# Eight weight low parts moved from GpSimd to VectorE, and an order for the accumulations, in an MLP of split fp32 products

## The chip, the cores and the metric

The kernel runs on one core of a Trainium2 chip. The metric is device time in microseconds for one execution of the program, from inputs in device memory to the output there. A core has TensorE (PE, matrix products into PSUM), VectorE (DVE), ScalarE (ACT), GpSimd (POOL) and SyncE (SP, which issues the DMAs here). Each engine takes its instructions in order; they wait for one another through semaphores.

## The reference

A decoder trunk of two layers on 512 tokens of width 1024, in fp32: a mixer (attention in layer 0, a gated short convolution in layer 1), an MLP and a gated embedding, each with RMSNorm before and after. The change lies in the MLP, which is the same in both layers:

```python
def sq_relu_mlp(h, w_up, w_down):
    return jnp.square(jax.nn.relu(h @ w_up)) @ w_down   # h 512x1024, w_up 1024x4096, w_down 4096x1024

def reference(...):
    for i in range(DEPTH):                              # DEPTH = 2
        ...
        f = sq_relu_mlp(rmsnorm(x, g[2]), w_mlp_up[i], w_mlp_down[i])
        x = x + rmsnorm(f, g[3])
        ...
```

## The kernel before

**Three products for one.** Every fp32 operand is split into a high part, rounded to the format in which TensorE multiplies, and a low part, the rest. ScalarE casts the high part (L272), another engine subtracts it from the source (L273). A product is then three matmuls, high x high (L264), low x high (L265) and high x low (L266), into the same PSUM bank. In the trace the names end in `h` and `l`: `wh`, `wl` for weights, `hTh`, `hTl` for the normed tokens, `A11h`, `A11l` and so on for activations. Which of the matmul's operands is streamed differs, so L265 is `wh` with an activation's low part in the down product and `wl` in the up product.

**Groups.** The 4096 hidden features go in eight groups of 512 (`gr` = 0 to 7), each of four tiles of 128 features (`f`). For each group `up` computes the up product, and ScalarE takes the relu `r` out of the bank (L820) and squares it into `q` (L806). In group 0 the up product runs in two passes of 256 tokens each, so that it can start before all tokens are normed; in the others in one pass of 512.

**Seven products for eight.** For groups 0 to 6 the down product is done with Strassen's seven products in Winograd's form, on 2 x 2 blocks: tokens by halves and hidden features by halves (f = 0, 1 and f = 2, 3) for the activations (A11, A12, A21, A22), hidden features and output columns for the weights (B11 to B22). It needs sums of the activations, S1 to S4, and of the weights, T1 to T4. The products are `PRODUCTS`, run in the order `STEPS`:

```python
PRODUCTS = {
    1: ("A11", "B11"), 2: ("A12", "B21"), 3: ("S4", "B22"), 4: ("A22", "T4"),
    5: ("S1", "T1"), 6: ("S2", "T2"), 7: ("S3", "T3"),
}
STEPS = (1, 2, 4, 5, 6, 7, 3)
```

- GpSimd makes the sums of the weights (`dn_T`, in `derive`, L167) from raw weights that a DMA loaded, T1, T3, T2, T4 for each of two feature tiles (`p` = 0, 1).
- `prepare` splits each weight: ScalarE casts, and the low part is taken by the engine that L185 chooses: GpSimd for every sum of weights in the MLP (keys that begin with `"dn"`), VectorE for plain weights.
- GpSimd makes the sums of the activations (`s`, in `quarters`, L834), for f = 1 and again for f = 3. ScalarE casts them (`S1h`, which holds S1 and S2, then `S3h`, which holds S3 and S4), and VectorE takes their low parts (`S1l`, `S3l`); `A12h` and `A12l` hold A12 and A22. These splits are made in `halves`.
- `down` runs the seven products, each for two halves of 128 tokens (`s` = 0, 1), each in a bank of its own. In group 0 ScalarE copies the banks into the accumulators `acc` (L863); in groups 1 to 6 VectorE adds the banks to `acc` (L866). Only then is a bank free. There are eight banks, taken in turn: the relu `r` of the last up tiles frees the banks for products 5, and the copy or addition of product 1 frees those for product 6.

**Order.** The program is written stage by stage, but outside of a few stretches written by hand a scheduler orders each engine's instructions by a simulated timeline. So an edit can move instructions of other engines, too. `tc.add_manual_dep` with `NoSync` gives the scheduler an order between two instructions of one engine, and adds no semaphore.

Of the kernel before, what the change touches and what calls it, by code (L numbers as in the profile page):

```python
# [8 lines left out]
F32 = mybir.dt.float32  # L9
F32R = mybir.dt.float32r  # L10
AF = mybir.ActivationFunctionType
ALU = mybir.AluOpType
# [42 lines left out]
ON_POOL = ('S3', 'S4')  # L55
# [13 lines left out]
def trunk(ctx: ExitStack, tc, x, pT, g, wv, wqk, bf, wo, wci, wcq, cw, wco, wup, wdn, wpp, wpg, out):  # L69
    nc = tc.nc  # L70
# [9 lines left out]
    def page(name, dtype=F32):  # L80
        return pages.tile([P, S], dtype, tag="pg", name=name)

    def bank(name):
        return psum.tile([P, S], F32, tag="ps", name=name)
# [66 lines left out]
    def fetch(upto):  # L151
        while len(fetched) < min(upto, len(loads)):
            n = len(fetched)
            raw = raws.tile([P, S], F32, tag="raw", name=f"raw{n}")
            fetched.append(raw)
            src = loads[n]
            nc.sync.dma_start(raw[:, : src.shape[-1]], src)

    def derive(key):
        at, sums = recipes.pop(key)  # L160
        fetch(max(at.values()) + 1)
        B = {name: fetched[n][:, :S] for name, n in at.items()}
        for name, a, b, op in sums:
            t = page("_".join(str(u) for u in (*key, *name)))
            derived[(*key, *name)] = t
            B[name] = t[:, :S]
            ins = nc.gpsimd.tensor_tensor(out=B[name], in0=B[a], in1=B[b], op=op)  # L167
            if last_norm:
                tc.add_manual_dep(
                    ins.ins, last_norm.pop().ins.name,  # L170
                    mybir.DependencyInfo(mybir.DependencyClass.Sync, mybir.DependencyReason.DATA),
                )

    def prepare(upto):
        while begun[0] < min(upto, len(order)):
            n = begun[0]
            begun[0] += 1
            key, at = order[n]
            for of in (key[:3], key[:2]):
                if of in recipes:  # L180
                    derive(of)
            hi, lo = page(f"wh{n}", F32R), page(f"wl{n}", F32R)
            if isinstance(at, tuple):
                raw, w = derived.pop(key), S
                eng = nc.gpsimd if key[0] == "dn" or key[-1] in ON_POOL else nc.vector  # L185
            else:
                fetch(at + 1)
                raw, eng, w = fetched[at], nc.vector, loads[at].shape[-1]
                fetched[at] = None
            split(hi[:, :w], lo[:, :w], raw[:, :w], eng)  # L190
            ready[key] = Pair(hi[:, :w], lo[:, :w])

    def wide(*key, soon=SOON):

        prepare(where[key] + 1 + soon)
        return ready[key]
# [6 lines left out]
    for l in range(2):  # L203
# [10 lines left out]
        else:  # L214
# [3 lines left out]
            for i in range(2, KT, 2):  # L218
                for name in "ucb":
                    s = "cub".index(name)  # L220
# [41 lines left out]
    def mm3(ps, a, b, start, stop):  # L262

        nc.tensor.matmul(ps, a.hi, b.hi, start=start, stop=False)  # L264
        nc.tensor.matmul(ps, a.lo, b.hi, start=False, stop=False)  # L265
        nc.tensor.matmul(ps, a.hi, b.lo, start=False, stop=stop)  # L266
        streamed[0] += 3 * ps.shape[-1]
        due()

    def split(hi, lo, src, eng=nc.vector):  # L270

        nc.scalar.copy(hi, src)  # L272
        eng.tensor_tensor(out=lo, in0=src, in1=hi.bitcast(F32), op=ALU.subtract)  # L273

    def gain(l, i):
        ts = [page(f"g{l}_{i}_{n}") for n in range(2)]
# [38 lines left out]
    def keep(t, n, ps, hT):  # L315
        to = lambda h: h[:, 4 * n : 4 * n + 4, t * P : (t + 1) * P]
        split(to(hT.hi), to(hT.lo), ps.rearrange("p (j c) -> p j c", j=4))
# [70 lines left out]
    def attention(hT, first_x, g0, by_hand):  # L388
# [8 lines left out]
        def logs():  # L397

            e, u, lg = stat("f_e", n_f), stat("f_u", n_f), stat("f_l", n_f)
            neg = stat("f_n", n_f)  # L400
            nc.vector.tensor_scalar(out=neg, in0=logit, scalar1=-1.0, scalar2=None, op0=ALU.mult)
            nc.vector.tensor_tensor(out=neg, in0=logit, in1=neg, op=ALU.min)
            nc.scalar.activation(e, neg, AF.Exp)
            nc.vector.tensor_scalar(out=u, in0=e, scalar1=1.0, scalar2=None, op0=ALU.add)
            nc.scalar.activation(lg, u, AF.Ln)
            rest, ru = stat("f_r", n_f), stat("f_ru", n_f)
            nc.vector.scalar_tensor_tensor(
                out=rest, in0=u, scalar=-1.0, in1=e, op0=ALU.add, op1=ALU.subtract
            )
            nc.vector.reciprocal(ru, u)  # L410
            nc.vector.tensor_tensor(out=rest, in0=rest, in1=ru, op=ALU.mult)
            nc.vector.tensor_tensor(out=lg, in0=lg, in1=rest, op=ALU.subtract)
            logf = stat("logf", n_f)
            nc.vector.scalar_tensor_tensor(
                out=logf, in0=logit, scalar=0.0, in1=lg, op0=ALU.min, op1=ALU.subtract
            )
            split(lf.hi, lf.lo, logf)
# [178 lines left out]
        def stream():  # L596
            for i in range(1, KT):
                yield from project(i)
            yield from out_part((0,), range(6))
            yield from out_part((1,), range(6))  # L600
            prepare(where["o", 1, KT - 1] + 1)
            yield from out_part((0, 1), (6,))
# [197 lines left out]
        return lambda k, t: tokens_of(ys[k], t)  # L800

    def mlp(l, hT, xs, then, late):
        acc = {}

        def square(out, r):
            nc.scalar.activation(out, r, AF.Square)  # L806
# [16 lines left out]
        def halves(gr, f, names, src, A):  # L823

            w = S // 2 * len(names)
            part = Pair(*(page(f"{names[0]}{s}{l}_{gr}_{f}", F32R) for s in "hl"))
            split(part.hi[:, :w], part.lo[:, :w], src[:, :w])
            for name, c in zip(names, (slice(0, S // 2), slice(S // 2, S))):
                A[name, f // 2] = part.at(lambda h: h[:, c])

        def quarters(gr, f, q, s, A):

            L, R = slice(0, S // 2), slice(S // 2, S)
            sums = lambda out, a, b, op: nc.gpsimd.tensor_tensor(out=out, in0=a, in1=b, op=op)  # L834
            if f % 2 == 0:
                s[f] = page(f"s34{l}_{gr}_{f}")
                sums(s[f][:, L], q[f][:, L], q[f][:, R], ALU.subtract)
                return
            left, right = q[f - 1], q[f]
            halves(gr, f, ("A12", "A22"), right, A)  # L840
            s12, s34 = page(f"s12{l}_{gr}_{f}"), s[f - 1]
            sums(s12[:, L], left[:, R], right[:, R], ALU.add)
            sums(s12[:, R], s12[:, L], left[:, L], ALU.subtract)
            sums(s34[:, R], right[:, L], s12[:, R], ALU.subtract)
            halves(gr, f, ("S1", "S2"), s12, A)
            halves(gr, f, ("S3", "S4"), s34, A)

        def down(gr, A):

            for i in STEPS:  # L850
                a_name, b_name = PRODUCTS[i]
                banks = [bank(f"dn{l}_{gr}_{i}{s}") for s in range(2)]
                for p in range(2):
                    w = wide("dn", l, gr, b_name, p)
                    for s in range(2):
                        mm3(
                            banks[s], A[a_name, p].at(lambda h: h[:, s * P : (s + 1) * P]), w,
                            p == 0, p == 1,
                        )
                for s in range(2):  # L860
                    if gr == 0:
                        acc[i, s] = page(f"acc{l}_{i}_{s}")
                        nc.scalar.copy(acc[i, s][:, :S], banks[s])  # L863
                    else:
                        a = acc[i, s][:, :S]
                        nc.vector.tensor_tensor(out=a, in0=banks[s], in1=a, op=ALU.add)  # L866

        def combine():

# [9 lines left out]
        for gr in range(7):  # L879
            A, s, q = {}, {}, {f: page(f"q{l}_{gr}_{f}") for f in range(4)}  # L880

            def done(f, lo, hi, r):
                square(q[f][:, lo:hi], r[:, : hi - lo])
                if lo == 0 and f % 2 == 0:
                    halves(gr, f, ("A11",), q[f], A)
                if hi == S:
                    quarters(gr, f, q, s, A)

            up(gr, done)
            down(gr, A)  # L890
# [16 lines left out]
        for t in range(NB):  # L907
            banks = [bank(f"dn{l}_7_{t}_{n}") for n in range(2)]
            for f, n in [(f, n) for f in range(4) for n in range(2)] if t == 0 else [
                (f, n) for n in range(2) for f in range(4)  # L910
            ]:
                w = wide("dn", l, 7, n, f, soon=14)
                mm3(banks[n], tokens_of(hs[f], t), w, f == 0, f == 3)
            for n in range(2):
                a = total[t, n][:, :S]
# [69 lines left out]
    for l in range(2):  # L985
# [16 lines left out]
        def late():  # L1002
# [6 lines left out]
            return g3  # L1009

        mlp(l, h2, xs, lambda t: pre_norm(t, xs[t], g4, hT, f"n4{l}"), late)
        h4 = hT
        g5 = gain(l, 5)
# [88 lines left out]
```

## Time and profile before

| | |
|---|---|
| median of 3 runs (lowest, highest) | 1234.35 us (1234.16, 1234.91) |
| the profiled execution: time, span | 1234.05 us, 1232.3 us |
| granted TensorE clock in it | 0.998 |
| instructions | 18654 |
| busy TensorE / VectorE | 1211.7 us (98%) / 898.9 us (73%) |
| busy ScalarE / GpSimd | 676.6 us (55%) / 680.3 us (55%) |

The span goes from the first to the last instruction of the program; the profiled execution's time is 1.75 us longer. Busy time of TensorE is a union of overlapping matmuls: where one starts before the last has ended, the distance of their starts tells how fast it runs, and not the duration of one. In the rows of a timeline the first number is the start in us from the start of the span, the second the time that the row covers; then engine, line, operation, output <- inputs, partitions x elements, and the number of instructions merged in the row. Brackets give the engine's idle time before the row, and whose work ended it. The MLP of layer 0 starts at about 259 us; group 0's down product runs from 285 to 306, group 1's from 328 to 348. Layer 1's follow some 570 us later.

### The profile page before, as it was taken

The page shows a single profiled execution, that of the slowest core. Times are in us where ns is not written, and L with a number is a line of the kernel's source. Part 1 is how long each engine was busy: PE and PEld are TensorE (multiplying, and loading weights), DVE is VectorE, ACT ScalarE, POOL GpSimd, SP SyncE. Part 2 cuts the span into 40 slices and gives each one's busy share as a digit, 9 for nine tenths or more (in the row PEclk, how much of TensorE's full clock was granted, in tenths as well). Part 3 has the DMA queues.
Part 4 walks back from the last instruction along what each step waited for, and adds up shares of the span by engine and source line. Part 5 has one row for each costly group of instructions (what it writes and reads, how often), then busy time and mean ns, then how long its engine had stood idle before and what let it go on. Part 6 is the DMA issues. An engine that isn't in the chain of part 4 may idle for free.

```text
span 1232.3 us, 18654 instructions
## 1 busy us (share of the span) xinstructions
PE 1211.7 (98%) x6188; PEld 1029.5 (84%) x6188; DVE 898.9 (73%) x1394; ACT 676.6 (55%) x1429; POOL 680.3 (55%) x635
## 2 busy tenths in 40 slices
PE   7999999999999999999999999999999999999997
PEld 6888888898788888888889999989878888888886
DVE  5658878675688767869877798865674787669873
ACT  5457778557634654455566534445756445635551
POOL 2016657147977787775213255317778868778210
PEclk9999999999999999999999999999999999999999
DMA  7456555532343224428123033552421443235401
GB/s 256 151 156 170 151 161 122 188 117 85 96 137 111 85 78 137 134 68 301 53 95 112 27 103 97 161 170 69 137 81 57 137 137 96 67 113 179 163 18 52
DMA packets 85793, 148.73 MB, mean 121 GB/s; under 512 B 10112, under 2 KB 17328, under 8 KB 85696
## 3 DMA queue, kind: packets, MB, share of 16 engines
q1 hardware_dynamic: 85488, 147.27, 39.0%
q8 instruction: 49, 0.80, 0.3%
q14 instruction: 48, 0.39, 0.1%
q10 hardware_dynamic: 144, 0.26, 0.1%
q0 software_dynamic: 64, 0.00, 0.0%
HBM read 136.93 MB, written 6.37 MB: 116 GB/s over the span
## 4 chain that ended last, share of the span: by engine, by line
PE 91%; DVE 3%; ACT 2%; POOL 2%; DMA 1%; issue 1%; SPq 0%; DVEq 0%; POOLq 0%; ACTq 0%
PE up L266 9%; PE up L265 9%; PE up L264 9%; PE dn L265 8%; PE dn L266 8%; PE dn L264 8%; PE qk L265 2%; PE qk L264 2%; PE qk L266 2%; PE pg L265 2%; PE pg L266 2%; PE pg L264 2%; PE pT L539 1%; PE n_p L312 1%; PE co L264 1%; PE co L265 1%
## 5 line engine op out<-in xcount | busy, mean ns | idle before, releaser
L273 DVE TENSOR_TENSOR wl<-raw,wh 128x512 fp32r<-128x512 f32 (+1 forms) x398 | 372.4, 980 | 27.3 <-ACT wh L272 26.2
L272 ACT CAST wh<-raw 128x512 fp32r<-128x512 f32 (+1 forms) x398 | 217.5, 619 | 4.6 <-DVE xd L348 4.4
L266 PE MATMUL up<-hTl,wh 128*128 128x512 f32 (+1 forms) x576 | 209.7, 366 | 0.6 <-DVE hTl L273 0.6
L265 PE MATMUL up<-hTh,wl 128*128 128x512 f32 (+1 forms) x576 | 210.2, 365 | 0.0
L264 PE MATMUL up<-hTh,wh 128*128 128x512 f32 (+1 forms) x576 | 209.4, 366 | 0.0
L273 POOL TENSOR_TENSOR wl<-dn_T,wh 128x512 fp32r<-128x512 f32 x112 | 154.7, 1414 | 32.6 <-ACT wh L272 32.6
L820 ACT ACTIVATE r<-up 128x512 f32<-128x512 f32 (+1 forms) x72 | 39.5, 548 | 199.2 <-PE up L266 199.2
L866 DVE TENSOR_TENSOR acc<-dn,acc 128x512 f32<-128x512 f32 x168 | 107.2, 679 | 23.5 <-PE dn L266 23.5
L266 PEld LDWEIGHTS up<-hTl,wh 128*128 128x128 f32 x576 | 108.3, 189 | 18.2 <-DVE hTl L273 0.8
L264 PEld LDWEIGHTS up<-hTh,wh 128*128 128x128 f32 x576 | 108.7, 189 | 17.6
L265 PEld LDWEIGHTS up<-hTh,wl 128*128 128x128 f32 x576 | 108.6, 189 | 17.5
L167 POOL TENSOR_TENSOR dn_T<-raw,raw 128x512 f32<-128x512 f32 x56 | 87.9, 1582 | 59.8 <-DMA raw<-in_wdn 49.7
L167 POOL TENSOR_TENSOR dn_T<-raw,dn_T 128x512 f32<-128x512 f32 x56 | 92.7, 1656 | 2.2
L272 ACT CAST wh<-dn_T 128x512 fp32r<-128x512 f32 x112 | 61.4, 616 | 11.1 <-POOL dn_T L167 11.1
L273 DVE TENSOR_TENSOR A12l<-q,A12h 128x512 fp32r<-128x512 f32 x28 | 23.6, 844 | 50.2 <-ACT A12h L272 50.2
L273 DVE TENSOR_TENSOR A11l<-q,A11h 128x256 fp32r<-128x256 f32 x28 | 25.6, 914 | 45.9 <-ACT A11h L272 45.9
L873 POOL TENSOR_TENSOR acc<-acc,acc 128x512 f32<-128x512 f32 x28 | 46.9, 1709 | 9.9 <-DVE acc L866 9.9
L265 PE MATMUL qk<-hTh,wl 128*128 128x512 f32 x128 | 51.0, 399 | 0.0
L266 PE MATMUL qk<-hTl,wh 128*128 128x512 f32 x128 | 51.0, 398 | 0.0
L264 PE MATMUL qk<-hTh,wh 128*128 128x512 f32 x128 | 50.9, 398 | 0.0
L265 PE MATMUL pg<-wh,hTl 128*128 128x512 f32 x128 | 50.5, 394 | 0.0
L264 PE MATMUL pg<-wh,hTh 128*128 128x512 f32 x128 | 50.4, 394 | 0.0
(370 smaller groups left out, 3231.5 us busy)
## 6 DMA issues: line engine op xcount, KB each, us to landing
raw<-in_wup SPq DMA_DIRECT2D x128, 256.0 KB, 3.1
raw<-in_wdn SPq DMA_DIRECT2D x128, 256.0 KB, 2.9
raw<-in_wcq SPq DMA_DIRECT2D x36, 256.0 KB, 2.8
raw<-in_wqk SPq DMA_DIRECT2D x32, 256.0 KB, 3.8
raw<-in_wpg SPq DMA_DIRECT2D x32, 256.0 KB, 4.6
g<-in_g SPq DMA_DIRECT2D x22, 256.0 KB, 6.2
prl<-neg_c SPq DMA_DIRECT2D x16, 256.0 KB, 7.0
raw<-in_wo SPq DMA_DIRECT2D x16, 256.0 KB, 5.8
```

The source lines that it names most:

```text
L167: ins = nc.gpsimd.tensor_tensor(out=B[name], in0=B[a], in1=B[b], op=op)
L264: nc.tensor.matmul(ps, a.hi, b.hi, start=start, stop=False)
L265: nc.tensor.matmul(ps, a.lo, b.hi, start=False, stop=False)
L266: nc.tensor.matmul(ps, a.hi, b.lo, start=False, stop=stop)
L272: nc.scalar.copy(hi, src)
L273: eng.tensor_tensor(out=lo, in0=src, in1=hi.bitcast(F32), op=ALU.subtract)
L312: nc.tensor.transpose(ps[:, j * P : (j + 1) * P], h[:, j * P : (j + 1) * P], ident)
L539: nc.tensor.transpose(ps[:, b * P : (b + 1) * P], probs[h][b][:, j * P : (j + 1) * P], ident)
L820: nc.scalar.activation(r[:, :n], ps[:, :n], AF.Relu)
L866: nc.vector.tensor_tensor(out=a, in0=banks[s], in1=a, op=ALU.add)
L873: nc.gpsimd.tensor_tensor(out=a, in0=a, in1=acc[i, s][:, :S], op=ALU.add)
```

## The change

Two edits, in both layers.

1. In `prepare`, the low parts of the sums of weights in group 0 (`key[2]` is the group) are taken by VectorE and no longer by GpSimd: T1 to T4, for two tiles each, eight instructions of 128 x 512 per layer. In groups 1 to 6 they stay on GpSimd.
2. `split` hands back its low part's instruction, and `halves` keeps the last one of each group (`lows[gr]`: the `S3l` of f = 3). In group 1 each of the 14 accumulations on VectorE is ordered behind it. Before, the scheduler had placed `A12l`, `S1l` and `S3l` of f = 3 between the accumulations of products 1, 2 and 4.

```diff
@@ prepare
-                eng = nc.gpsimd if key[0] == "dn" or key[-1] in ON_POOL else nc.vector
+                eng = nc.gpsimd if (key[0] == "dn" and key[2] > 0) or key[-1] in ON_POOL else nc.vector
@@ split
         nc.scalar.copy(hi, src)
-        eng.tensor_tensor(out=lo, in0=src, in1=hi.bitcast(F32), op=ALU.subtract)
+        return eng.tensor_tensor(out=lo, in0=src, in1=hi.bitcast(F32), op=ALU.subtract)
@@ mlp
-        acc = {}
+        acc, lows = {}, {}
@@ halves
-            split(part.hi[:, :w], part.lo[:, :w], src[:, :w])
+            lows[gr] = split(part.hi[:, :w], part.lo[:, :w], src[:, :w])
@@ down
                         a = acc[i, s][:, :S]
-                        nc.vector.tensor_tensor(out=a, in0=banks[s], in1=a, op=ALU.add)
+                        ins = nc.vector.tensor_tensor(out=a, in0=banks[s], in1=a, op=ALU.add)
+                        if gr == 1:
+                            tc.add_manual_dep(
+                                ins.ins, lows[gr].ins.name,
+                                mybir.DependencyInfo(
+                                    mybir.DependencyClass.NoSync, mybir.DependencyReason.DATA
+                                ),
+                            )
```

## The prediction

> **What bounds the kernel now.** I read the page first, then the chain of waits, and then the timeline of each engine around the two groups that the diff touches. The page's first part:
>
> ```profile
> span 1232.3 us, 18654 instructions
> PE 1211.7 (98%) x6188; PEld 1029.5 (84%) x6188; DVE 898.9 (73%) x1394; ACT 676.6 (55%) x1429; POOL 680.3 (55%) x635
> ```
>
> TensorE is the bound. Nothing done on VectorE, ScalarE or GpSimd can shorten the kernel except where TensorE stands still for it. So the question is how many such places there are in the first two MLP groups, and how long they are. In the timeline the first column is the start, the second the duration, and brackets give the idle time before and who ended it. TensorE, down products of group 0, layer 0 and then layer 1:
>
> ```profile
> 290.27 0.39 PE L266 MATMUL dn<-wl,A12h 128*128 128x512 f32 x1
> 291.58 0.50 PE L264 MATMUL dn<-wh,S1h 128*128 128x512 f32 x1 [0.92 <-ACT r L820]
> 292.87 0.39 PE L266 MATMUL dn<-wl,S1h 128*128 128x512 f32 x1
> 293.41 0.73 PE L264 MATMUL dn<-wh,A12h 128*128 128x512 f32 x2 [0.15 <-ACT A12h L272]
> 297.39 0.39 PE L266 MATMUL dn<-wl,S1h 128*128 128x512 f32 x1
> 297.72 0.50 PE L264 MATMUL dn<-wh,S1h 128*128 128x512 f32 x1
> 861.35 0.39 PE L266 MATMUL dn<-wl,A12h 128*128 128x512 f32 x1
> 861.98 0.50 PE L264 MATMUL dn<-wh,S1h 128*128 128x512 f32 x1 [0.24 <-ACT r L820]
> 863.27 0.40 PE L266 MATMUL dn<-wl,S1h 128*128 128x512 f32 x1
> 863.80 0.73 PE L264 MATMUL dn<-wh,A12h 128*128 128x512 f32 x2
> ```
>
> Matmuls overlap: a steady one shows 0.39 but the next starts about 0.23 later (below, three starting at 334.81 end at 335.65, so 0.84 = 2 x 0.23 + 0.39). The loss is therefore the distance of two starts less 0.23, and more than the bracket says. The first after a halt takes 0.50 instead of 0.39, another 0.11. Layer 0 loses 1.08, 0.31 and 0.10, each with 0.11: 1.82 us. Layer 1 loses 0.40 and 0.30, with 0.11 each: 0.92. Group 1, both layers:
>
> ```profile
> 334.81 0.84 PE L264 MATMUL dn<-wh,A12h 128*128 128x512 f32 x3
> 335.79 0.50 PE L265 MATMUL dn<-wh,A12l 128*128 128x512 f32 x1
> 337.75 0.61 PE L264 MATMUL dn<-wh,S1h 128*128 128x512 f32 x2
> 338.75 0.50 PE L265 MATMUL dn<-wh,S1l 128*128 128x512 f32 x1 [0.39 <-DVE S1l L273]
> 339.79 0.39 PE L264 MATMUL dn<-wh,S1h 128*128 128x512 f32 x1
> 905.22 0.84 PE L264 MATMUL dn<-wh,A12h 128*128 128x512 f32 x3
> 906.43 0.50 PE L265 MATMUL dn<-wh,A12l 128*128 128x512 f32 x1 [0.37 <-DVE A12l L273]
> 908.39 0.63 PE L264 MATMUL dn<-wh,S1h 128*128 128x512 f32 x2
> 909.39 0.50 PE L265 MATMUL dn<-wh,S1l 128*128 128x512 f32 x1 [0.38 <-DVE S1l L273]
> ```
>
> Three matmuls from 334.81 make the next due at 335.50; it came at 335.79: 0.29. Two from 337.75 make the next due at 338.21; it came at 338.75: 0.54. With 0.11 each, layer 0 loses 1.05. Layer 1, in the same way, 0.52 + 0.54 + 0.22 = 1.28. Group 1 loses 2.33 us in all.
>
> **Edit 1: eight low parts per layer from GpSimd to VectorE (group 0).** In the built order GpSimd drops two runs of four `wl`; VectorE takes the first four between the `A11l` of f = 0 and that of f = 2, the other four behind `S3l` of f = 3. ScalarE's and SyncE's orders stay as they are, so no cast and no DMA issue is moved. What that does to the path is read from ScalarE, GpSimd and VectorE:
>
> ```profile
> 286.55 0.42 ACT L806 ACTIVATE q<-r 128x256 f32<-128x256 f32 x1
> 289.80 0.62 ACT L272 CAST S1h<-s 128x512 fp32r<-128x512 f32 x1 [2.18 <-POOL s L834]
> 292.29 0.42 ACT L806 ACTIVATE q<-r 128x256 f32<-128x256 f32 x1
> 294.71 0.62 ACT L272 CAST S1h<-s 128x512 fp32r<-128x512 f32 x1 [1.35 <-POOL s L834]
> 856.93 0.42 ACT L806 ACTIVATE q<-r 128x256 f32<-128x256 f32 x1
> 860.20 0.62 ACT L272 CAST S1h<-s 128x512 fp32r<-128x512 f32 x1 [2.19 <-POOL s L834]
> 862.68 0.42 ACT L806 ACTIVATE q<-r 128x256 f32<-128x256 f32 x1
> 865.11 0.62 ACT L272 CAST S1h<-s 128x512 fp32r<-128x512 f32 x1 [1.36 <-POOL s L834]
> ```
> ```profile
> 278.75 3.18 POOL L167 TENSOR_TENSOR dn_T<-raw,dn_T 128x512 f32<-128x512 f32 x2
> 281.88 5.24 POOL L273 TENSOR_TENSOR wl<-dn_T,wh 128x512 fp32r<-128x512 f32 x4
> 287.08 0.74 POOL L834 TENSOR_TENSOR s<-q 128x256 f32<-128x256 f32 x1
> ```
> ```profile
> 275.85 3.48 DVE L273 TENSOR_TENSOR wl<-raw,wh 128x512 fp32r<-128x512 f32 x2
> 279.25 1.51 DVE L273 TENSOR_TENSOR A11l<-q,A11h 128x256 fp32r<-128x256 f32 x1
> 284.81 1.15 DVE L273 TENSOR_TENSOR A11l<-q,A11h 128x256 fp32r<-128x256 f32 x1 [4.05 <-ACT A11h L272]
> 296.18 0.69 DVE L273 TENSOR_TENSOR S3l<-s,S3h 128x512 fp32r<-128x512 f32 x1
> 300.72 1.63 DVE L273 TENSOR_TENSOR wl<-raw,wh 128x512 fp32r<-128x512 f32 x1 [3.85 <-ACT wh L272]
> ```
>
> The chain goes: GpSimd does four `wl` until about 287.1, and only then its sums `s`; ScalarE, in order, stands at the cast `S1h` for them; behind that cast are queued `S3h` and the relu `r` of the next up bank; TensorE waits at 291.58 for just that bank. Take the four `wl` away and `s` waits for `q` alone. What that is worth I read from the second pass of the same code (f = 3), where GpSimd is free: from the end of `q` (292.29 + 0.42 = 292.71) to `S1h` at 294.71 it takes 2.00 us. In the first pass (f = 1) it takes 289.80 - 286.97 = 2.83. Gain 0.83. In layer 1: 2.01 (863.10 to 865.11) against 2.85 (857.35 to 860.20). Gain 0.84.
>
> All that follows on ScalarE in this group moves with it, as its order is fixed: the relus, the casts `A12h` (TensorE's wait at 293.41) and the copies `acc` that free the banks (297.72). In layer 0 the first halt shrinks by 0.83 and the two others stay: gain 0.83. In layer 1 the first halt (0.40) goes, and the rest of the 0.84 comes out of the second: gain 0.84. Sum of edit 1: 1.67 us.
>
> Its cost: eight low parts at 0.69 (the `S3l` row) are 5.5 us of VectorE per layer. The first four need 2.8 in a gap that runs from 280.76 (279.25 + 1.51) to 284.81, 4.05 long; the last four 2.8 in one from 296.87 to 300.72, 3.85 long. I price them at nothing: the gaps cover them. If the cover were gone the next low part would be late by what sticks out. One thing is not covered: GpSimd's last `dn_T` now has a `wl` on VectorE beside it. Side by side both engines run at the same pace (two `wl` in 3.48), and two `dn_T` took 3.18 here, so it might stretch by up to 0.30, and ScalarE, which stands at the cast of that `dn_T`, with it. Between 0 and 0.30 per layer I take 0: this `dn_T` started before the `A11l` ended, so its turn came ahead of any later `wl`. The Trainium skill (SBUF — State Buffer, section "SBUF: two separate sides") says that a GpSimd operation and a VectorE one with two SBUF inputs hold a shared port in turn, each for its whole instruction, whoever starts first; by that rule the term is 0 here, by the pace of the rows up to 0.30, so the sum would be 4.0 or 3.4. The equal pace in the rows agrees with it.
>
> **Edit 2: accumulations of group 1 behind `S3l`.** VectorE now stands idle for a matmul while finished inputs wait behind:
>
> ```profile
> 333.65 1.29 DVE L866 TENSOR_TENSOR acc<-dn,acc 128x512 f32<-128x512 f32 x2 [5.19 <-PE dn L266]
> 332.67 0.62 ACT L272 CAST S3h<-s 128x512 fp32r<-128x512 f32 x1 [0.21 <-POOL s L834]
> ```
>
> It is idle 5.19 us until product 1 is complete, adds it twice, and only then takes up `A12l`; the next accumulation again holds up `S1l`. In the new order all three low parts lie in that idle time: the last cast, `S3h`, ends at 333.29, so `S3l` ends by about 334.0, and TensorE wants `A12l` at 335.50 and `S1l` at 338.21 (334.7 and 337.0 once edit 1 and the first two halts are off), `S3l` later. All four halts go: 2.33 us. What is added is that the accumulations wait for `S3l`: the first starts at 334.0 instead of 333.65, 0.35 late. Behind it are the other accumulations and the `wl` of the next up weights; for its bank waits product 6, whose first matmul was at 339.79. Even brought forward by 1.9 (0.83 and 1.05) that is 337.9, almost 4 us after that start. So no cost. The built order also pulls a few first matmuls of group 2's up product forward over rests of products 7 and 3; nothing is added, and what they read was cast long before. No cost, and bounded by the 2.33 that this edit gives.
>
> **Sum.** 1.67 + 2.33 = 4.00 us off the profiled execution's 1234.05 (span 1232.3) gives 1230.05; the median 1234.35 is 0.3 above that execution, so 1230.3, or 0.33% faster. What a measurement of this kernel can tell from no change is 0.2%, 2.5 us.
>
> **Rivals.**
> - *VectorE takes the port first.* If the first moved `wl` runs ahead of the last `dn_T`, ScalarE is held up by 0.69 in each layer, and edit 1 keeps 0.29: 1231.7. The equal pace, one each in turn, speaks against it. Chance 0.07.
> - *Edit 1 gains nothing*, because ScalarE's next wait ends as late as before: 1234.35 - 2.33 = 1232.0. Against it: in the second pass nothing else ended later. Chance 0.05.
> - *Edit 2 gains nothing*, since a bank's release by the later accumulations takes the place of the low parts: 1232.7. Against it: 4 us of slack. Chance 0.06.
> - *Both work and a later stage takes it back*, as something that TensorE does not pace (weights by DMA) sets a later start: 1234.3. For it: SyncE's order is unchanged. Against it: TensorE at 98%, and the tail hangs on TensorE. Chance 0.06.
> - *VectorE becomes the bound (slower).* If the moved low parts run at the shared pace of 1.74 (3.48 for two), the second four start at 296.87 and end at 303.8, less the 0.83 of the earlier start 303.0, 2.3 past the 300.72 at which the next weights' `wl` began, and TensorE waits. It decides once they end past 300.72 and TensorE has no slack left. Price 2 x 2.3 less edit 2's 2.33: +2.3, 1236.6; where the backlog reaches group 1's low parts too, 1238.9. For it: VectorE is the second busiest engine. Against it: GpSimd, relieved of the same work, has nothing to contend with there. Chance 0.08, counted as slower.
>
> That the change does nothing is no case: the orders of both engines do differ as the diff says.
>
> **Numbers.** Forecast as summed: chance 0.68, at 1230.3. Its own range runs from 1229.0 (all of 1.82 + 0.92 + 2.33 = 5.07 gone, and a little more where layer 1 has a third halt) to 1230.9 (0.30 lost in each layer). The range 1228.8 to 1232.7 takes in the first three rivals and leaves out the last two, 0.14. Faster by over 0.2% is below 1231.9: 0.68 + 0.07 = 0.75. Within 0.2%: 0.05 + 0.06 + 0.06 = 0.17. Slower: 0.08.
>
> **What would show it.** Right: in group 0 GpSimd's first `s` starts within 0.1 us of the end of `q`, `S1h` about 2.0 after that `q`, and TensorE's first halt is some 0.25 in layer 0 and gone in layer 1; in group 1 no matmul starts more than 0.25 after the one before it, and `acc` follows `S3l`. Wrong: a `dn_T` of group 0 that grew to 1.7, a TensorE wait named `acc` or `wl` in groups 0 to 2, or TensorE's idle time turning up again after group 2.

## The result, and the profile after

The changed kernel takes 1229.85 us (median of 6 runs, 1229.41 to 1230.79) against 1234.26 (6 runs, 1233.08 to 1235.06): a ratio of 0.9967, with a 95% interval of 0.9956 to 0.9978. The profiled execution took 1230.79, the slowest of its six. The span of that execution is 1229.1 us. From the page of the changed kernel, the engines:

```profile
PE 1210.3 (98%) x6188; PEld 1030.5 (84%) x6188; DVE 912.2 (74%) x1410; ACT 676.4 (55%) x1429; POOL 657.1 (53%) x619
```

VectorE has 16 operations more and GpSimd 16 fewer, and TensorE's busy time is 1.4 us less; what changed is where it stands still. Group 0 in TensorE's timeline of the changed kernel, layer 0 and then layer 1 (start, duration, engine, line, operation; brackets: idle before and who ended it):

```profile
291.22 0.39 PE L266 MATMUL dn<-wl,A12h 128*128 128x512 f32 x1
291.67 0.50 PE L264 MATMUL dn<-wh,S1h 128*128 128x512 f32 x1
292.95 0.40 PE L266 MATMUL dn<-wl,S1h 128*128 128x512 f32 x1
293.49 1.19 PE L264 MATMUL dn<-wh,A12h 128*128 128x512 f32 x4
297.48 0.39 PE L266 MATMUL dn<-wl,S1h 128*128 128x512 f32 x1
297.80 0.50 PE L264 MATMUL dn<-wh,S1h 128*128 128x512 f32 x1
861.64 0.39 PE L266 MATMUL dn<-wl,S1h 128*128 128x512 f32 x1
861.88 1.20 PE L264 MATMUL dn<-wh,A12h 128*128 128x512 f32 x4
865.87 0.39 PE L266 MATMUL dn<-wl,S1h 128*128 128x512 f32 x1
866.19 0.50 PE L264 MATMUL dn<-wh,S1h 128*128 128x512 f32 x1
```

Read as in the prediction (the distance of two starts less 0.227 us, at which matmuls follow one another without a halt), layer 0's first halt fell from 1.08 to 0.22, its second stayed at 0.31 and its third at 0.10; each has its 0.11 for the first matmul behind it besides. In layer 1 the first halt is gone, of the second only the 0.11 is left, and the third is 0.10. Group 1, in the same two places as before:

```profile
334.66 1.07 PE L264 MATMUL dn<-wh,A12h 128*128 128x512 f32 x4
335.56 0.39 PE L265 MATMUL dn<-wh,A12l 128*128 128x512 f32 x1
337.38 0.62 PE L264 MATMUL dn<-wh,S1h 128*128 128x512 f32 x2
337.83 0.39 PE L265 MATMUL dn<-wh,S1l 128*128 128x512 f32 x1
903.09 1.07 PE L264 MATMUL dn<-wh,A12h 128*128 128x512 f32 x4
904.00 0.39 PE L265 MATMUL dn<-wh,A12l 128*128 128x512 f32 x1
```

Four matmuls from 334.66 make the next due at 335.57 (4 x 0.227), and it comes at 335.56. There is no halt left in group 1.

On the engines behind it: the ends of `q` and the casts `S1h` on ScalarE, GpSimd's sums, VectorE's low parts, and VectorE's order in group 1:

```profile
287.46 0.42 ACT L806 ACTIVATE q<-r 128x256 f32<-128x256 f32 x1
289.89 0.62 ACT L272 CAST S1h<-s 128x512 fp32r<-128x512 f32 x1 [1.35 <-POOL s L834]
```
```profile
279.67 3.18 POOL L167 TENSOR_TENSOR dn_T<-raw,dn_T 128x512 f32<-128x512 f32 x2
287.24 0.74 POOL L834 TENSOR_TENSOR s<-q 128x256 f32<-128x256 f32 x1 [4.39 <-ACT q L806]
```
```profile
281.62 3.81 DVE L273 TENSOR_TENSOR wl<-dn_T,wh 128x512 fp32r<-128x512 f32 x4
285.74 0.42 DVE L273 TENSOR_TENSOR A11l<-q,A11h 128x256 fp32r<-128x256 f32 x1 [0.31 <-ACT A11h L272]
332.94 0.69 DVE L273 TENSOR_TENSOR S3l<-s,S3h 128x512 fp32r<-128x512 f32 x1
333.72 1.29 DVE L866 TENSOR_TENSOR acc<-dn,acc 128x512 f32<-128x512 f32 x2
```

From the end of `q` to `S1h` it is now 289.89 - 287.88 = 2.01 us, and 2.00 in layer 1; it was 2.83 and 2.85. GpSimd, idle for 4.39 us, now waits for `q`. The four moved low parts end just before the next `A11l`, and the accumulations of group 1 follow `S3l`.

### The profile page after: what moved, and what is told of

Its sections match the earlier page's. It is cut to its first block, busy times and chain, and to the rows that moved or that the text cites. A ratio compares the mean times of both kernels' runs of the same rounds, so it can differ in the third digit from the quotient of the medians.

```text
span 1229.1 us, 18662 instructions
## 1 busy us (share of the span) xinstructions
PE 1210.3 (98%) x6188; PEld 1030.5 (84%) x6188; DVE 912.2 (74%) x1410; ACT 676.4 (55%) x1429; POOL 657.1 (53%) x619
## 4 chain that ended last, share of the span: by engine, by line
PE 96%; ACT 1%; DVE 1%; DMA 1%; issue 1%; POOL 1%; SPq 0%; DVEq 0%; POOLq 0%; ACTq 0%
PE up L266 9%; PE up L265 9%; PE up L264 9%; PE dn L264 8%; PE dn L265 8%; PE dn L266 8%; PE qk L265 2%; PE qk L264 2%; PE qk L266 2%; PE pg L265 2%; PE pg L264 2%; PE pg L266 2%; PE n_p L312 1%; PE pT L539 1%; PE v L264 1%; PE v L265 1%
## 5 line engine op out<-in xcount | busy, mean ns | idle before, releaser
L273 DVE TENSOR_TENSOR wl<-raw,wh 128x512 fp32r<-128x512 f32 (+1 forms) x398 | 377.3, 991 | 22.3 <-ACT wh L272 21.3
L273 POOL TENSOR_TENSOR wl<-dn_T,wh 128x512 fp32r<-128x512 f32 x96 | 132.6, 1413 | 30.1 <-ACT wh L272 30.1
L273 DVE TENSOR_TENSOR A11l<-q,A11h 128x256 fp32r<-128x256 f32 x28 | 23.1, 825 | 36.5 <-ACT A11h L272 36.5
```

What stands on the lines that cost most here:

```text
L273: return eng.tensor_tensor(out=lo, in0=src, in1=hi.bitcast(F32), op=ALU.subtract)
```

## The experiments

For each kernel I added up TensorE's halts in its one profiled execution, as above, in the four places that the change touches, over the matmuls of 128 x 512 and for distances that exceed 0.227 us by more than 0.025. The sections below tell what each kernel is; every time is a median.

| kernel | group 0, layer 0 | group 1, layer 0 | group 0, layer 1 | group 1, layer 1 | sum, us | less than before, us | time, us | before beside it, us | less than before, us |
|---|---|---|---|---|---|---|---|---|---|
| before | 1.87 | 1.08 | 1.16 | 1.29 | 5.39 | | | 1234.26 | |
| the change | 0.96 | 0 | 0.32 | 0 | 1.28 | 4.11 | 1229.85 | 1234.26 | 4.41 |
| edit 1 alone | 1.02 | 1.50 | 0.32 | 1.97 | 4.80 | 0.59 | 1232.78 | 1234.07 | 1.29 |
| edit 2 alone | 1.82 | 0 | 1.18 | 0 | 3.00 | 2.39 | 1232.00 | 1234.07 | 2.07 |
| edit 1, first four | 1.00 | 1.03 | 0.31 | 1.30 | 3.64 | 1.75 | 1232.61 | 1234.07 | 1.46 |
| edit 1, second four | 1.84 | 1.44 | 1.18 | 1.71 | 6.17 | -0.78 | 1234.91 | 1234.07 | -0.84 |
| low parts of all groups | 0.97 | 0 | 0.31 | 0 | 1.29 | 4.10 | 1229.73 | 1234.16 | 4.43 |
| low parts of groups 0 and 1 | 0.98 | 0 | 0.32 | 0 | 1.30 | 4.09 | 1229.95 | 1234.16 | 4.21 |
| ScalarE's order | 0.55 | 0 | 0 | 0 | 0.55 | 4.84 | 1229.13 | 1234.16 | 5.03 |
| new order in all groups | 0.98 | 0 | 0.32 | 0 | 1.31 | 4.08 | 1229.84 | 1234.16 | 4.32 |
| first four and edit 2 | 0.96 | 0 | 0.33 | 0 | 1.28 | 4.11 | 1230.02 | 1234.18 | 4.16 |
| no sharing in group 1 | 0.99 | 0.30 | 0.33 | 0.30 | 1.92 | 3.47 | 1230.55 | 1234.18 | 3.63 |
| ScalarE's order, second form | 0.11 | 0 | 0 | 0 | 0.11 | 5.28 | 1228.58 | 1234.18 | 5.60 |

The halts tell the time of each kernel within 0.35 us but for edit 1 alone (0.7 off). An interval of a ratio is about 0.001 to either side, some 1.2 us, so small differences rest on the halts, which repeat to a few hundredths from kernel to kernel where the edits leave a place alone.

**Edit 1 alone.** The accumulations stand in their old order:

```diff
-                        if gr == 1:
+                        if False:
```

> The first edit alone: the low parts of group 0's weight sums on VectorE, group 1's accumulations in their old order. If the halts of TensorE are the whole account, group 0's halts are those of the changed kernel (0.96 us in layer 0 and 0.32 in layer 1, from 1.87 and 1.18) and group 1's are those of before (1.08 and 1.29), so the time is before less about 1.8: 1232.5 us, and the gain adds with that of the second edit alone to the whole change's 4.4. Rival: the two edits lean on each other (VectorE, with more to do in group 0, comes later to group 1), so group 1's halts grow and the time is within 0.5 us of before.

1232.78 us, a ratio of 0.9987 (0.9978 to 0.9996). Group 0 is as in the changed kernel, and the gain there is 0.85 + 0.84 = 1.69 us by the halts. But group 1 halts for 1.50 and 1.97 us, 0.42 and 0.68 more than before. Of the 1.69 edit 1 keeps 0.59 by the halts. By the medians it keeps 1.29, and their interval (0.5 to 2.7) holds both; the profiled execution took 1233.60, 0.45 less than that of the kernel before (1234.05). So it is the halts, and not the times, that show the loss. The rival was right that the two edits lean on each other; its reason, VectorE coming late to group 1, was not. VectorE, GpSimd and TensorE in group 1 of layer 0 in this kernel:

```profile
332.81 1.29 DVE L866 TENSOR_TENSOR acc<-dn,acc 128x512 f32<-128x512 f32 x2 [6.00 <-PE dn L266]
334.01 1.33 DVE L273 TENSOR_TENSOR A12l<-q,A12h 128x512 fp32r<-128x512 f32 x1
336.78 1.51 DVE L273 TENSOR_TENSOR S1l<-s,S1h 128x512 fp32r<-128x512 f32 x1
```
```profile
332.23 5.51 POOL L273 TENSOR_TENSOR wl<-dn_T,wh 128x512 fp32r<-128x512 f32 x4 [1.25 <-ACT wh L272]
333.48 1.31 POOL L273 TENSOR_TENSOR wl<-dn_T,wh 128x512 fp32r<-128x512 f32 x1
```
```profile
333.74 1.07 PE L264 MATMUL dn<-wh,A12h 128*128 128x512 f32 x4
335.39 0.50 PE L265 MATMUL dn<-wh,A12l 128*128 128x512 f32 x1 [0.58 <-DVE A12l L273]
```

VectorE waits 6.00 us for product 1, so it is not late. `A12l` needs 1.33 where `S3l` of group 0 took 0.69 in the kernel before, and ends at 335.34, 0.55 after the end of GpSimd's second `wl` (333.48 + 1.31 = 334.79). The same part in the kernel before, and GpSimd's `wl` beside it:

```profile
334.86 0.88 DVE L273 TENSOR_TENSOR A12l<-q,A12h 128x512 fp32r<-128x512 f32 x1
```
```profile
333.89 1.30 POOL L273 TENSOR_TENSOR wl<-dn_T,wh 128x512 fp32r<-128x512 f32 x1 [1.25 <-ACT wh L272]
```

There GpSimd's first `wl` ends at 335.19, and `A12l` again 0.55 later, at 335.74. So `A12l` lasts the rest of the GpSimd operation that it meets, and 0.55 more. Before, the four `wl` began 0.24 us after the first accumulation (333.65), and `A12l` met the end of the first; in this kernel they begin 0.58 ahead of it (332.23 against 332.81), and `A12l` meets the second.

**Edit 2 alone.** All eight low parts back on GpSimd:

```diff
-                eng = nc.gpsimd if (key[0] == "dn" and key[2] > 0) or key[-1] in ON_POOL else nc.vector
+                eng = nc.gpsimd if key[0] == "dn" or key[-1] in ON_POOL else nc.vector
```

> The second edit alone: group 1's accumulations behind its low parts, group 0's weight sums as before. By the halts, group 1 has none in either layer and group 0 keeps 1.87 and 1.18: before less 2.4, 1231.9 us. Rival: the accumulations that are put off are handed back to group 2, whose matmuls then halt: within 0.5 us of before, with a halt named in group 2.

1232.00 us, 0.9982 (0.9973 to 0.9991). Group 1 has no halt, group 0 has its old ones, and none appeared in group 2. By the halts edit 2 is worth 2.39 us by itself. The rival falls.

**The halves of edit 1.** The first four `wl` (T4 and T1) stand ahead of the sums on GpSimd, the other four (T2 and T3) behind those of f = 3. The condition in L185, cut out of its line, with a comment added:

```diff
-(key[0] == "dn" and key[2] > 0)
+(key[0] == "dn" and (key[2] > 0 or key[3] in ("T2", "T3")))   # first four on VectorE
+(key[0] == "dn" and (key[2] > 0 or key[3] in ("T4", "T1")))   # second four on VectorE
```

> Of the first edit only the four low parts that stand ahead of the activations' sums (T4 and T1), on VectorE; the other four stay on GpSimd, and group 1 is as before. If only what is queued ahead of the sums on GpSimd counts, this has the whole gain of the first edit: as that edit alone, about 1232.5 us, POOL's first sum within 0.1 us of the end of q in group 0. Rival: GpSimd's load in the whole group counts, then half of it: about 1233.4.

> Of the first edit only the four low parts that stand behind the activations' sums (T2 and T3), on VectorE; the other four stay on GpSimd, ahead of the sums, and group 1 is as before. If only the queue ahead of the sums counts, the first sum starts as late as before (0.83 us after q's end) and the time is that of before, within 0.4 us. Rival: half of the first edit's gain, about 1233.4.

1232.61 us (0.9987, 0.9979 to 0.9996) and 1234.91 us (1.0004, 0.9995 to 1.0013). The whole gain in group 0 belongs to the first four: 1.00 and 0.31 us of halts, against 1.84 and 1.18 with the second four. The second four bring nothing there, and group 1's halts grow only with them (1.44 and 1.71, against 1.03 and 1.30). Without four `wl` behind its sums, GpSimd comes earlier to the next group: its four `wl` of group 1 begin at 333.24, 0.64 ahead of the first accumulation (333.88), as in edit 1 alone; with the first four only they begin at 333.19, 0.19 behind it (333.00).

The way there leads through a DMA. GpSimd's first sum of weights for group 1 waits for raw weights in each of these kernels, and SyncE issues their DMA when VectorE's first `wl` from raw weights has ended. In the kernel before, this `wl` (300.72, 1.63 us) meets the last of GpSimd's four, which end at 296.75 + 5.05 = 301.80, and ends 0.55 after it. With the second four on VectorE nothing is beside it, and it takes 0.69, to 301.65. SyncE and GpSimd, in the kernel before and then in the one with the second four:

```profile
302.38 2.13 SPq L157 DMA_DIRECT2D raw<-in_wdn  x4
305.12 1.47 POOL L167 TENSOR_TENSOR dn_T<-raw,raw 128x512 f32<-128x512 f32 x1 [3.32 <-DMA raw<-in_wdn]
```
```profile
301.68 2.95 SPq L157 DMA_DIRECT2D raw<-in_wdn  x4
304.35 1.29 POOL L167 TENSOR_TENSOR dn_T<-raw,raw 128x512 f32<-128x512 f32 x1 [8.62 <-DMA raw<-in_wdn]
```

The DMA goes out 0.70 earlier and the sum starts 0.77 earlier, though `S3l` of group 0 stands 0.24 later in this trace (296.42 against 296.18). From the kernel with the second four, VectorE in group 1:

```profile
333.88 1.29 DVE L866 TENSOR_TENSOR acc<-dn,acc 128x512 f32<-128x512 f32 x2 [6.08 <-PE dn L266]
335.09 1.24 DVE L273 TENSOR_TENSOR A12l<-q,A12h 128x512 fp32r<-128x512 f32 x1
```

Neither forecast for the second four had a loss; by the halts it is 0.78 us, while the ratio's interval holds no change.

**First four and edit 2.** If so, the second four are of no use in the change either:

> The changed kernel with T2 and T3 of group 0 back on GpSimd: the first four low parts on VectorE, and group 1's new order. The second four alone made group 1's halts grow (by 0.36 and 0.42 us in the two layers). Theory: they bring nothing in group 0, and what they cost in group 1 the new order takes away, so without them the time is the changed kernel's: group 0's halts 0.97 and 0.32 us, group 1's none, 1229.9 us within 0.4. Rival: with the order in place the second four bring something of their own: 1230.5 us or more without them.

1230.02 us, 0.9963 (0.9951 to 0.9976), with the changed kernel's halts in each place. Four of the eight moved low parts are enough. What the other four cost in group 1 is hidden by edit 2, which lets VectorE take `A12l` well ahead of its need.

**Sharing taken away in group 1.** Edit 1 alone, and T2 and T3 of group 1 on VectorE too. There they stand behind `S3l`, and GpSimd has nothing to do beside `A12l` and `S1l`; TensorE's halts then show what VectorE's old order costs by itself:

```diff
-(key[0] == "dn" and key[2] > 0)
+(key[0] == "dn" and not (key[2] == 0 or (key[2] == 1 and key[3] in ("T2", "T3"))))
```

> The first edit alone, group 1's accumulations in their old order, and besides that T2 and T3's low parts of group 1 on VectorE, where they come behind the activations' low parts, so that GpSimd runs nothing beside these. With the first edit alone A12l of the second pair took 1.33 us in layer 0 and 1.78 in layer 1, and S1l 1.51 and 1.53, each with such a low part on GpSimd beside it; alone an op of this form takes 0.69. Theory (the growth of group 1's halts, and most of these halts themselves, is the time in which VectorE waits for GpSimd's op to end): both take 0.69, the halts of 0.75 and 0.52 us in layer 0 and 1.20 and 0.55 in layer 1 fall to about 0.1 and 0 in each, and the time is 3.0 us below that of the first edit alone: 1229.8, though no accumulation was moved. Rival (only the two accumulations ahead of A12l count): the halts stay at 0.3 to 0.5 us, as before the change, and the time is at 1232 to 1233.

1230.55 us, 0.9969 (0.9957 to 0.9981). VectorE and TensorE in group 1:

```profile
333.33 0.68 DVE L273 TENSOR_TENSOR A12l<-q,A12h 128x512 fp32r<-128x512 f32 x1
335.44 0.68 DVE L273 TENSOR_TENSOR S1l<-s,S1h 128x512 fp32r<-128x512 f32 x1
```
```profile
333.06 1.07 PE L264 MATMUL dn<-wh,A12h 128*128 128x512 f32 x4
334.07 0.50 PE L265 MATMUL dn<-wh,A12l 128*128 128x512 f32 x1
336.02 0.62 PE L264 MATMUL dn<-wh,S1h 128*128 128x512 f32 x2
336.47 0.39 PE L265 MATMUL dn<-wh,S1l 128*128 128x512 f32 x1
```

With the accumulations in the old order `A12l` takes 0.68 instead of 1.33, its halt falls from 0.75 to 0.10, and the one for `S1l` is gone. Both were predicted in size; a third, of 0.09 between two matmuls with a moved `wl` (due at 339.42), was not. Group 1 keeps 0.30 of 1.50 and of 1.97 us, which takes 2.88 us of halts off edit 1 alone; the median is 2.2 lower, where 3.0 was expected. So most of its halts was VectorE's wait for GpSimd, and the order of the accumulations decided when the low parts met GpSimd's work and how much room there was.

**More on VectorE.** In place of group 0's low parts those of groups 0 and 1, and of all seven groups:

```diff
-(key[0] == "dn" and key[2] > 0)
+(key[0] == "dn" and key[2] > 1)   # groups 0 and 1; without this clause: all groups
```

> The changed kernel, with group 1's weight sums' low parts on VectorE too. Theory: group 1 has no halts left to remove, so within 0.4 us of the changed kernel, 1229.9. Rival: the moved low parts stand ahead of group 1's activations' low parts on VectorE and put S1l and S3l off by 0.69 us each that lies before them: a halt of 0.5 to 1.5 us in group 1 of each layer, 1231 to 1233.

> The changed kernel, with the weight sums' low parts of all seven groups of each layer on VectorE instead of group 0's alone: 96 more on VectorE, 0.68 us each, 65 us of its time, which then goes from 912 us (74% of the span) to about 980 (80%). Theory: from group 2 on TensorE has no halts, and VectorE has room in a group of some 41 us, so the time is that of the changed kernel, 1229.9, or a few tenths above where a low part of the weights comes late. Rival: VectorE becomes the bound in the middle groups: its queue delays the accumulations, TensorE waits for banks, and the time is 3 us or more above, with PE halts in groups 2 to 6.

1229.95 us (0.9967, 0.9955 to 0.998) and 1229.73 (0.9967, 0.9954 to 0.9979), both with the changed kernel's halts. The page of the kernel with all groups on VectorE:

```profile
PE 1210.1 (99%) x6188; PEld 1029.8 (84%) x6188; DVE 948.1 (77%) x1506; ACT 676.6 (55%) x1429; POOL 534.5 (44%) x523
```

VectorE does not become the bound with 96 operations more, six times the change's 16. Its busy time grew by 36 us and not by the 65 I had worked out, while GpSimd's fell by 123. VectorE's busy time holds its waits for GpSimd, and there are fewer: the time by which its low parts of 128 x 512 exceed 0.69 each adds up to 142 us in the changed kernel and to 121 here. The rest of the difference is that operations in a row overlap, with 0.60 from start to start.

**The new order in all groups.** `if gr == 1:` becomes `if True:`.

> The changed kernel, with the order of group 1 (accumulations behind the low parts) in all groups from 1 to 6. Theory: no halts stand there to be removed, and none are added: within 0.4 us of the changed kernel, 1229.9. Rival: accumulations put off hold PSUM banks longer, so TensorE waits for a bank in each group: slower by 0.5 us or more, with halts in groups 2 to 6 that name an acc.

1229.84 us, 0.9967 (0.9955 to 0.9979), with no halt in groups 1 to 6: nothing gained, nothing lost.

**What is left in group 0.** Its first halt is still ScalarE standing at `S1h` of f = 1 while the relus and `q` of the second pair wait behind it. `halves` gets an `after`, and in group 0 the casts of f = 1 are put behind the last `q`:

```diff
+            if gr == 0 and f == 1:
+                held.extend([(("S1", "S2"), s12), (("S3", "S4"), s34)])
+                return
...
+                if hi == S and f == 3:
+                    while held:
+                        halves(gr, 1, *held.pop(0), A, after=last)
```

> The changed kernel, with ScalarE's casts S1h and S3h of the first pair of group 0 put behind the last q of the second pair. The halts that are left are 0.96 us in layer 0 and 0.32 in layer 1, where the second pair's S1h ends 2.00 us after its q. Theory: with q of the second pair earlier on ScalarE, its sums and its casts come earlier, and the time falls by 0.6 to 1.3 us: 1228.6 to 1229.3. Rival: the casts put off make the first pair's high and low parts late, S1l by some 0.35 us or more, and TensorE halts there instead: within 0.3 us of the changed kernel, or above it, with a halt that waits for a high or a low part of the first pair.

1229.13 us, 0.9962 (0.995 to 0.9975). Layer 1 has no halts left, layer 0 has 0.55 us: the theory holds at its lower end. What is left is the rival's effect in small: 0.09 behind the first matmul with the first pair's `S1l`, and 0.34 + 0.11 at `A12l` of the second pair, which the first pair's low parts hold up. VectorE and TensorE of this kernel:

```profile
290.87 1.01 DVE L278 TENSOR_TENSOR S3l<-s,S3h 128x512 fp32r<-128x512 f32 x1
291.80 1.22 DVE L278 TENSOR_TENSOR A12l<-q,A12h 128x512 fp32r<-128x512 f32 x1
```
```profile
290.35 0.61 PE L264 MATMUL dn<-wh,S1h 128*128 128x512 f32 x2
293.08 0.50 PE L265 MATMUL dn<-wh,A12l 128*128 128x512 f32 x1 [0.17 <-DVE A12l L278]
```

`A12l` stands behind `S3l`, which TensorE wants later. The second form takes `S3h` off the hold only after `A12h` of f = 3:

```diff
-                    while held:
+                    if held:
                         halves(gr, 1, *held.pop(0), A, after=last)
...
             halves(gr, f, ("A12", "A22"), right, A)
+            if held:
+                halves(gr, 1, *held.pop(0), A)
```

> ScalarE's order of the earlier run (the casts S1h and S3h of group 0's first pair behind the last q), with A12h of the second pair now between S1h and S3h, so that VectorE takes A12l ahead of S3l. The earlier order left 0.09 us ahead of a matmul of S1 and 0.34 + 0.11 us ahead of one that waits for A12l, all in layer 0; A12l stood behind S1l (1.26 us) and S3l (1.01 us) on VectorE and ended at 293.02 us. Theory: A12l starts about 290.8 and is done some 1.4 us earlier, that halt goes, S3l comes late enough for nothing: 1229.13 less 0.45, 1228.7 us. Rival: S3l or the second pair's S1l, put off by A12l, ends too late and a halt of 0.3 us or more takes its place: 1229.1 or above.

1228.58 us, 0.9953 (0.9941 to 0.9966), the best of all. Both halts are gone; one restart of 0.11 us is left. `A12l` now runs ahead of `S3l`:

```profile
291.43 1.22 DVE L278 TENSOR_TENSOR A12l<-q,A12h 128x512 fp32r<-128x512 f32 x1
292.58 1.22 DVE L278 TENSOR_TENSOR S3l<-s,S3h 128x512 fp32r<-128x512 f32 x1
```
```profile
291.17 0.62 PE L264 MATMUL dn<-wh,S1h 128*128 128x512 f32 x2
291.62 1.07 PE L264 MATMUL dn<-wh,A12h 128*128 128x512 f32 x4
292.52 0.39 PE L265 MATMUL dn<-wh,S1l 128*128 128x512 f32 x1
293.43 0.39 PE L265 MATMUL dn<-wh,A12l 128*128 128x512 f32 x1
```

This stage stands 0.8 us later in this trace than in that of the first form, so I count from the first matmul with `S1h`. In the first form `A12l` ended 293.02 - 290.35 = 2.67 us after it, here 292.65 - 291.17 = 1.48: 1.19 earlier, where 1.4 was expected.

The scheduler also moved four matmuls of `A12h` ahead of those of `S1l` on TensorE. That gives `S1l` 0.9 us more, but `A12l` nothing: in both forms ten matmuls, 2.27 us, run from that first matmul to the one that wants `A12l`. So the 0.34 + 0.11 went by VectorE's order. The 0.09 behind `S1l` is gone too; whether by this order or by TensorE's isn't told apart.

## Why the prediction was right

**TensorE as the bound, halts as the currency: right.** The halts removed are 4.11 us, and the median fell by 4.41. The two spans differ by 3.2 and not by 4.1; this execution of the changed kernel waited longer outside the MLP (TensorE's wait named `n_p` 1.8 us instead of 0.8, that for the first row 6.4 instead of 6.0).

**Edit 1's gain in group 0, 1.67: right.** Measured 0.91 + 0.84 = 1.75 with edit 2 and 1.69 without, by the chain that was given: `S1h` 2.01 and 2.00 us after `q`. The third halt of layer 1, which the prediction left out, stays.

**Edit 1's cost of nothing: wrong for edit 1 alone.** The step that failed is the cover. The gaps do hold the moved low parts, as priced; but it asked what the eight do to VectorE and to group 0, and not what their absence on GpSimd does to group 1. That no DMA issue is moved holds for their order alone: the raw weights of group 1 are issued at 301.52 in the changed kernel, against 302.38, though `S3l` of group 0 stands 0.08 later there. GpSimd reaches group 1 earlier, and its `wl` there meet `A12l` at a worse moment: 1.10 us of new halts, which by the halts cost edit 1 alone two thirds of its gain. The sum still came out because edit 2 takes away all of group 1's halts, old and new. That was luck, as the prediction had no term for the new ones. The terms could not simply be added: apart the two edits give 0.59 + 2.39 = 2.98 by the halts, together 4.11 (by the medians 1.29 + 2.07 = 3.36, together 4.41).

**The last `dn_T`, 0 to 0.30: 0, as taken.** Two took 3.18 us, as before. The moved `wl` paid instead: four took 3.81, where four at the pace of the last three (0.69, the next 0.60 later) take 2.5.

**Edit 2's gain, 2.33: right, 2.37 and 2.39.** Its explanation was half of it. VectorE stood idle for an accumulation while `A12l` was ready, as the prediction said; but in the old order with nothing on GpSimd beside them the late low parts cost 0.2 us a layer, not 1.08 and 1.29.

**The rivals.** VectorE taking the port first did not occur: `dn_T` was not stretched. Edit 2 was not eaten by later banks, in group 1 or where it was put on all groups. VectorE as the bound is far off. "A later stage takes it back" is in part what happened to edit 1 by itself, one group on. The weights' DMA has a hand in it, but as it comes earlier, not as a later start.

## What to carry to other kernels

Work taken off an engine changes when that engine does its next work; so look one stage on for whom it then meets, not only at the engine that takes the work over. Test the parts of a change singly before adding their gains: here, by the halts, one part was worth a third of what it seemed until the other was there, and half of it was worth nothing. On a saturated engine count halts by the distances of starts; they separate versions that the times cannot.

## What the runs showed of the hardware

**A low part on VectorE that starts while a GpSimd operation runs ended 0.55 us after that operation, whenever it had started.** `A12l` in layer 0 of edit 1 alone (1.33 us) and of the kernel before (0.88), 0.55 in both; alone it takes 0.69. The moved `wl` in the changed kernel from 281.62 took 1.77 us as one operation, to 283.39, 0.54 after the end of `dn_T` (279.67 + 3.18 = 282.85):

```profile
281.62 1.77 DVE L273 TENSOR_TENSOR wl<-dn_T,wh 128x512 fp32r<-128x512 f32 x1
```

The Trainium skill (SBUF — State Buffer, section "SBUF: two separate sides") states it as a lock: of a GpSimd operation and a VectorE one with two SBUF inputs, the one that starts first holds the shared port for its whole length, and the other waits. The trace agrees, by the 0.55 above.

**Accumulations are not held up.** In edit 1 alone two accumulations, with one input from PSUM, ran from 332.81 in 1.29 us while GpSimd's `wl` ran from 332.23; the two took 1.29 as well in the kernel without sharing in group 1, where GpSimd had no `wl` beside them, and GpSimd's second `wl`, 1.31, was not stretched either. The two SBUF inputs in the rule of the Trainium skill above (SBUF — State Buffer, section "SBUF: two separate sides") fit that. In this kernel an accumulation can be put beside GpSimd's work where a low part can't.
